# Gate and up of three feed-forward chunks by seven block products, with the sums on GpSimd

## The chip, the core and the metric

One core of a Trainium2 chip runs the whole kernel. Its engines work side by side: TensorE (PE: matrix products into PSUM; PEld is its weight load), VectorE (DVE) and ScalarE (ACT) for what comes out of PSUM and for preparing operands, GpSimd (POOL) for small things that lie in SBUF, SyncE (SP) for most of the DMA issues. The metric is the device time of one execution in microseconds.

## The reference

Two layers, each a feed-forward block, a mixer and a second feed-forward block, over 256 rows of 1024 in fp32. The mixers (latent attention with a recurrence in layer 0, differential attention in layer 1) stand outside the change. What the change touches:

```python
def swiglu(x, w_gate, w_up, w_down):
    return (jax.nn.silu(x @ w_gate) * (x @ w_up)) @ w_down

for l in range(DEPTH):
    g = norm_g[l]
    h = swiglu(rms_norm(x, g[0, 0]), ffn_w_gate[l, 0], ffn_w_up[l, 0], ffn_w_down[l, 0])
    x = x + 0.5 * rms_norm(h, g[0, 1])
    ...                                   # the mixer
    h = swiglu(rms_norm(x, g[2, 0]), ffn_w_gate[l, 1], ffn_w_up[l, 1], ffn_w_down[l, 1])
    x = x + 0.5 * rms_norm(h, g[2, 1])
```

`w_gate` and `w_up` are 1024 x 2816, `w_down` 2816 x 1024, different in each of the four blocks.

## The kernel before

The 256 rows are two tiles of 128. A product in fp32 is made of three TensorE instructions on split operands: every operand is the sum of a high part `hi` and a low part `lo`, both of type fp32r, and `mm3` (L242) issues hi x hi, hi x lo, lo x hi. The stationary operand is the transposed activation of a tile (`xT[t]`, hi and lo, for gate and up; `hT[t]` for down), the moving operand 512 columns of a weight.

**Weight stream.** Weights come in one packed array in the order of use, cut into units and these into subunits of 128 x 1024 (for gate and up two k tiles of 512 columns). `emit_load` (L197) issues for each subunit the DMA into a `raw` buffer (SP's queue; 5 buffers, L175 `wraw`), ScalarE's copy raw to `whi` (L219) and VectorE's `wlo = raw - whi` (L224), and chains the low parts so that they run in this order. In a feed-forward block split subunits lie in a pool of 7 buffers (`fw`, L422, `BUFS_F`); a mixer's, and the first of a following block, in one of 5 (`wsp`). A buffer is free again when the last product that reads it is done. `fill` (L256) keeps the stream up to seven subunits ahead of what the products have taken.

**A feed-forward block** (`ffn`, L430) runs over six chunks of the 2816 columns, of 512, 512, 256, 512, 512, 512. Each chunk multiplies both tiles by gate (`group`, L263: a subunit serves tile 0 and then tile 1, 12 instructions), evicts with silu on ScalarE (L440), multiplies by up, and forms `h` on VectorE (`gated`, L445). The transposes of the previous chunk's `h` (`turn`, L448, split by ScalarE L360 and VectorE L361) stand between gate and up, the products of the previous chunk with `w_down` behind up. The first chunk (`group_first`, L275) works on tile 0 first, because the norm and the transposes of tile 1 (`post_norm` L376, `turn_x` L363) are still under way; the down products of the last two chunks (the tail) are ordered so that the first tile's norm and transposes run beside the second tile's products.

**PSUM** is eight banks: four (`y`) hold the running down sums, four (`w`) rotate for everything else. GpSimd's work is the powers of the norms (L343, L388) and some products of the mixers. Instructions of an engine run in the order that the scheduler of the framework gave them; an engine waits at the head of its queue.

## Time and profile before

| what | us |
|---|---|
| runs | 1028.34, 1028.74, 1030.66 |
| median | 1028.74 |
| span of the profiled execution | 1027.8 |
| TensorE busy in it | 1011.3 |
| VectorE, ScalarE, GpSimd busy | 625.8, 517.1, 49.9 |

The span counts from the first to the last instruction of the execution that the hardware profiler took. In the rows further down, `L244` is a line of the program, `out<-in` are the program's tile names, `x` behind an entry is a count; what stands in brackets is the idle time of the engine just before an instruction and what ended it. Busy times of TensorE are modelled ends of pipelined instructions, so the distance between starts is the better measure of its pace.

### The profile page before, as it was taken

Reading aid. Unit: us, or ns where it says so; the run is one execution under the profiler, and the core shown is the slowest. Engines: PE = TensorE matmul, PEld = TensorE weight load, DVE = VectorE, ACT = ScalarE, POOL = GpSimd, SP = SyncE. Lnnn points to the kernel's source line nnn. Section 1 sums busy time; section 2 is a strip of 40 time slices with the busy share of each in tenths; the row PEclk is TensorE's granted clock in tenths of the full one; section 3 lists DMA queues with packets and bytes.
Section 4 is the critical chain, followed back from the end, with each engine's and each line's share of the span. In section 5 each row is a group of like instructions: output and inputs, shape, how many; then the busy total and the mean of one; then the engine's idle time right before and its main releaser. Section 6 shows DMA issues by size and latency. Waiting matters only on the chain.

```text
span 1027.8 us, 13158 instructions
## 1 busy us (share of the span) xinstructions
PE 1011.3 (98%) x4979; PEld 843.5 (82%) x4979; DVE 625.8 (61%) x876; ACT 517.1 (50%) x757; POOL 49.9 (5%) x61
## 2 busy tenths in 40 slices
PE   8999999999999999999999999999999999999997
PEld 6888888888788889888888888888877878888886
DVE  6555585768577855455576555546676786455553
ACT  6544455477644644444554444444665565444441
POOL 1000000021201000000000000000011200000000
PEclk8999999999999999999999999999999999999999
DMA  8765555575221765555547555555634366655531
GB/s 282 271 202 186 186 184 189 180 225 194 86 81 58 253 212 196 185 184 187 182 164 246 187 183 189 191 190 168 208 121 147 102 206 225 201 182 189 186 123 41
DMA packets 51903, 184.25 MB, mean 179 GB/s; under 512 B 6136, under 2 KB 6528, under 8 KB 51840
## 3 DMA queue, kind: packets, MB, share of 16 engines
q1 hardware_dynamic: 48960, 176.05, 51.8%
q10 hardware_dynamic: 2880, 7.37, 2.1%
q8 instruction: 39, 0.64, 0.2%
q14 instruction: 24, 0.20, 0.1%
HBM read 182.35 MB, written 1.05 MB: 178 GB/s over the span
## 4 chain that ended last, share of the span: by engine, by line
PE 90%; DVE 4%; issue 3%; ACT 1%; DMA 1%; POOL 1%; SPq 0%; DVEq 0%; POOLq 0%; ACTq 0%
PE w L244 16%; PE w L246 16%; PE w L245 16%; PE y L246 9%; PE y L244 9%; PE y L245 9%; PE w L292 7%; PE w L353 2%; DVE wlo L224 1%; PE y L353 1%; DMA raw<-in_w_dram 1%; ACT whi L219 1%; POOL pm L1007 0%; DVE E L857 0%; DVE pm L1009 0%
## 5 line engine op out<-in xcount | busy, mean ns | idle before, releaser
L224 DVE TENSOR_TENSOR wlo<-raw,whi 128x1024 fp32r<-128x1024 f32 (+2 forms) x331 | 404.0, 1227 | 283.6 <-ACT whi L219 281.2
L219 ACT CAST whi<-raw 128x1024 fp32r<-128x1024 f32 (+1 forms) x331 | 345.0, 1049 | 365.5 <-PE w L246 206.6
L244 PE MATMUL w<-whi,xThi 128*128 128x512 f32 (+1 forms) x836 | 315.6, 377 | 0.0
L246 PE MATMUL w<-whi,xTlo 128*128 128x512 f32 (+1 forms) x836 | 312.0, 373 | 0.0
L245 PE MATMUL w<-wlo,xThi 128*128 128x512 f32 (+1 forms) x836 | 311.5, 373 | 0.0
L246 PEld LDWEIGHTS w<-whi,xTlo 128*128 128x128 f32 x836 | 157.3, 188 | 28.3 <-issue 0.3
L244 PEld LDWEIGHTS w<-whi,xThi 128*128 128x128 f32 x836 | 157.5, 188 | 27.5 <-issue 1.0
L245 PEld LDWEIGHTS w<-wlo,xThi 128*128 128x128 f32 x836 | 157.5, 188 | 26.4
L244 PE MATMUL y<-whi,hThi 128*128 128x512 f32 x352 | 138.4, 393 | 0.0
L246 PE MATMUL y<-whi,hTlo 128*128 128x512 f32 x352 | 137.2, 390 | 0.0
L245 PE MATMUL y<-wlo,hThi 128*128 128x512 f32 x352 | 137.1, 389 | 0.0
L246 PEld LDWEIGHTS y<-whi,hTlo 128*128 128x128 f32 x352 | 66.1, 188 | 14.0
L245 PEld LDWEIGHTS y<-wlo,hThi 128*128 128x128 f32 x352 | 66.1, 188 | 13.2
L244 PEld LDWEIGHTS y<-whi,hThi 128*128 128x128 f32 x352 | 66.1, 188 | 13.2
L361 DVE TENSOR_TENSOR hTlo<-w,hThi 128x512 fp32r<-128x512 f32 (+1 forms) x48 | 29.1, 640 | 34.0 <-ACT hThi L360 34.0
L440 ACT ACTIVATE s<-w,sm 128x512 f32<-128x512 f32 (+1 forms) x48 | 31.4, 653 | 25.9 <-PE w L246 20.3
L388 POOL TENSOR_TENSOR sm<-sm,mhalf 128x1 f32<-128x1 f32 x12 | 6.6, 550 | 726.6 <-DVE sm L386 726.6
L292 PE MATMUL w<-whi,xThi 128*128 128x512 f32 (+2 forms) x124 | 39.1, 397 | 2.6 <-ACT xThi L360 2.6
L292 PE MATMUL w<-wlo,xThi 128*128 128x512 f32 (+2 forms) x124 | 37.8, 389 | 0.4 <-DVE wlo L224 0.4
L292 PE MATMUL w<-whi,xTlo 128*128 128x512 f32 (+2 forms) x124 | 37.9, 390 | 0.0
L445 DVE SCALAR_TENSOR_TENSOR h<-w,sm,s 128x512 f32<-128x512 f32 (+1 forms) x48 | 32.0, 699 | 0.7 <-PE w L246 0.5
L292 PEld LDWEIGHTS w<-whi,xThi 128*128 128x128 f32 x124 | 22.6, 192 | 6.6 <-ACT xThi L360 3.1
(246 smaller groups left out, 820.2 us busy)
## 6 DMA issues: line engine op xcount, KB each, us to landing
raw<-in_w_dram SPq DMA_DIRECT2D x325, 512.0 KB, 3.6
g<-in_norm_g_dram ACTq DMA_DIRECT2D x9, 512.0 KB, 4.6
raw<-in_w_dram SPq DMA_DIRECT2D x4, 448.0 KB, 3.4
g<-in_norm_g_dram SPq DMA_DIRECT2D x2, 512.0 KB, 6.2
out_dram<-x SPq DMA_DIRECT2D x4, 256.0 KB, 2.1
E<-in_hw_dram ACTq DMA_DIRECT2D x1, 576.0 KB, 6.7
x<-in_x_dram SPq DMA_DIRECT2D x2, 256.0 KB, 3.0
x<-in_x_dram SPq DMA_DIRECT2D x1, 512.0 KB
```

Of the source, the lines that this page charges most:

```text
L219: c = nc.scalar.copy(hi[:, :w], raw[:, :w])
L224: state["lo"] = nc.vector.tensor_tensor(lo[:, :w], raw[:, :w], hi[:, :w].bitcast(F32), op=ALU.subtract)
L244: mm(ps, hi[:, j, :], rhi, start=start, stop=False)
L245: mm(ps, hi[:, j, :], rlo, start=False, stop=False)
L246: state["mm"] = mm(ps, lo[:, j, :], rhi, start=False, stop=stop)
L292: state["mm"] = mm(o, lhs[:, k, :], rhs[:, i, :], start=j == 0 and k == 0, stop=j == 2 and k == KD - 1)
L353: nc.tensor.transpose(ps[:, i * P:(i + 1) * P], src[:, (b + i) * P:(b + i + 1) * P], ident)
L361: return c, nc.vector.tensor_tensor(lo.rearrange("p a b -> p (a b)"), ps, h2.bitcast(F32), op=ALU.subtract)
L388: nc.gpsimd.tensor_tensor(r, v, mhalf[:, :1], op=ALU.pow)
L440: nc.scalar.activation(s[:, :w], ps[:, :w], AF.Silu, scale=r[t])
L445: nc.vector.scalar_tensor_tensor(hh[:, :w], ps[:, :w], r[t], s[:, :w], op0=ALU.mult, op1=ALU.mult)
```

## The change

In chunks 1, 3 and 5 of each block the four products (tile 0, tile 1) x (gate, up) over 1024 rows of weight are seen as a product of two 2 x 2 block matrices: A11, A12 are the first and second half (512) of tile 0's columns, A21, A22 of tile 1's; B11, B21 the halves of gate, B12, B22 of up. Eight block products of 12 instructions become seven (Winograd's form), with sums of blocks as operands:

- operand sums, once a block: S1 = A21 + A22, S2 = S1 - A11, S3 = A11 - A21, S4 = A12 - S2, made on GpSimd from hi + lo (4 additions, 4 sums), then split by ScalarE's copy and GpSimd's subtraction. S1 and S2 lie in `oT`, S3 and S4 in new tiles.
- weight sums, per chunk: T1 = B12 - B11, T2 = B22 - T1, T3 = B11 - T2, T4 = B21 - T2, each as two GpSimd operations on 128 x 1024 raw weights, written over a raw buffer that is no longer needed. They go through the same split as a loaded subunit, so a chunk has 14 subunits to split, not 8, of which each serves one product of 6 instructions.
- the products in the order X = A11 B11, W = S1 T1, X += S2 T2, Y = A12 B21, X += S3 T3, X += A22 T4, W += S4 B22. ScalarE copies X to SBUF after the first, second and third product on it (`held`), VectorE adds Y or W to these copies (`plus`). tile 0's gate is X's first state + Y, tile 0's up the second + W, tile 1's up the third + W as it stands before S4 B22 is added, tile 1's gate X's last state.

The seven's raw weights get a pool of 8 buffers (`RAWS`), the feed-forward blocks' split buffers fall from 7 to 4 and alternate with the 5 of `wsp` (`RING`). Half of the previous chunk's down products stand between T3 and T4 (in the last such chunk none).

```diff
-BUFS_F = 7
+BUFS_F = 4
+SEVEN = (1,3,5)
+RAWS = 8
+RING = "wfwfwfwfw"
 ...
+        if ci in SEVEN:
+            gate, up = ([("ffn_w_" + n, (l, j), k, 4, [(a, a + w)]) for k in (0, 4)] for n in ("gate", "up"))
+            pa, pw = starts[ci - 1]
+            d = [("ffn_w_down", (l, j), f, 2, [(0, D)]) for f in range(pa // P, (pa + pw) // P, 2)]
+            half = (len(d) + 1) // 2 if ci < len(CHUNKS) - 1 else 0
+            units += [gate[0] + ("B11",), up[0] + ("T1",), up[1] + ("T2",), gate[1] + ("B21",), (None, None, 0, 4, [(a, a + w)], "T3")]
+            units += d[:half] + [(None, None, 0, 4, [(a, a + w)], "T4"), (None, None, 0, 4, [(a, a + w)], "B22")] + d[half:]
+            continue
 ...
     def emit_load():
 ...
+                raw = (wraw if kind is None else state["raws"]).tile([P, SPLIT], F32, name="raw", tag="raw")
+                moved = nc.sync.dma_start(raw[:, :w], src[:, k * nc_:k * nc_ + w])
 ...
+                sub = nc.gpsimd.tensor_tensor
+                if kind in ("B11", "B21"):
+                    kept[kind, k] = raw
+                elif kind == "T1":
+                    sub(raw, raw, kept["B11", k], op=ALU.subtract)
+                    kept["T", k] = raw
+                elif kind == "T2":
+                    kept["B22", k] = raw
+                    sub(kept["T", k], raw, kept["T", k], op=ALU.subtract)
+                    raw = kept["T", k]
+                elif kind == "T3":
+                    raw = kept["B11", k]
+                    sub(raw, kept["T", k], raw, op=ALU.subtract)
+                elif kind == "T4":
+                    raw = kept["B21", k]
+                    sub(raw, raw, kept["T", k], op=ALU.subtract)
+                else:
+                    raw = kept["B22", k]
+            pool, tag = wsp, "w"
+            if ours:
+                if RING[state["turn"] % len(RING)] == "f":
+                    pool, tag = state["pool"], "f"
+                state["turn"] += 1
 ...
+            def row_sums(fp):
+                xf = [cp.tile([P, D], F32, name="xf", tag="c") for _ in range(NT)]
+                A = [[xf[t][:, 512 * i:512 * i + 512] for i in range(2)] for t in range(NT)]
+                tt = nc.gpsimd.tensor_tensor
+                for t in range(NT):
+                    for i in range(2):
+                        hi, lo = (v.rearrange("p k n -> p (k n)").bitcast(F32) for v in half(t, i))
+                        tt(A[t][i], hi, lo, op=ALU.add)
+                tt(A[1][1], A[1][0], A[1][1], op=ALU.add)
+                tt(A[1][0], A[0][0], A[1][0], op=ALU.subtract)
+                tt(A[0][0], A[1][1], A[0][0], op=ALU.subtract)
+                tt(A[0][1], A[0][1], A[0][0], op=ALU.subtract)
 ...
+                for v, dst in zip((A[1][1], A[0][0], A[1][0], A[0][1]), (oT[0], oT[1], *more)):
+                    hi, lo = (d.rearrange("p k n -> p (k n)") for d in dst)
+                    nc.scalar.copy(hi, v)
+                    tt(lo, v, hi.bitcast(F32), op=ALU.subtract)
 ...
+            def seven(ci):
 ...
+                X = bank()
+                prod(X, half(0, 0), True)
+                hT = [turn(0, CHUNKS[ci - 1]), None]
+                W = bank()
+                prod(W, S1, True)
+                p1 = held(X)
+                hT[1] = turn(1, CHUNKS[ci - 1])
+                prod(X, S2, False)
+                Y = bank()
+                prod(Y, half(0, 1), True)
+                u2 = held(X)
+                s0 = silu(0, plus(p1, Y), 512)
+                prod(X, S3, False)
+                downs(range(kf))
+                u3 = held(X)
+                c22 = plus(u3, W)
+                prod(X, half(1, 1), False)
+                s1 = silu(1, X, 512)
+                prod(W, S4, False)
+                h = [gated(0, plus(u2, W), s0, 512), gated(1, c22, s1, 512)]
+                downs(range(kf, wp))
 ...
+            sums = row_sums(fp)
             for ci in range(1, nch):
                 w, wp = CHUNKS[ci], CHUNKS[ci - 1]
+                if ci in SEVEN:
+                    seven(ci)
+                    continue
 ...
-    nc = _bacc.Bacc("TRN2", target_bir_lowering=False, num_devices=1)
+    nc = _bacc.Bacc("TRN2", target_bir_lowering=False, num_devices=1, dynamic_dma_scratch_size=512)
```

## Rows read from the trace of the kernel before

**Rows 1.** Page, part 1: busy time, share of the span, instructions of each engine.

```profile
PE 1011.3 (98%) x4979; PEld 843.5 (82%) x4979; DVE 625.8 (61%) x876; ACT 517.1 (50%) x757; POOL 49.9 (5%) x61
```

**Rows 2.** Page, part 4: the chain that ended last, by engine.

```profile
PE 90%; DVE 4%; issue 3%; ACT 1%; DMA 1%; POOL 1%; SPq 0%; DVEq 0%; POOLq 0%; ACTq 0%
```

**Rows 3.** Timeline, TensorE: start us, us, engine, line, operation, operands, count.

```profile
553.50 0.39 PE L244 MATMUL w<-whi,xThi 128*128 128x512 f32 x1
...
576.18 0.39 PE L244 MATMUL y<-whi,hThi 128*128 128x512 f32 x1
...
587.06 0.28 PE L244 MATMUL w<-whi,xThi 128*128 128x256 f32 x1
```

**Rows 4.** Busy time by stretch, third feed-forward block: length, engines, clock, DMA.

```profile
553.50:587.10 33.60, 33.60 (x154) 27.89 (x153) 19.75 (x19) 15.18 (x17) 0.00 (x0) 1.00 0.66 222
587.10:610.20 23.10, 23.10 (x153) 21.25 (x152) 11.88 (x12) 10.22 (x12) 0.00 (x0) 1.00 0.55 181
...
638.00:671.50 33.50, 33.50 (x153) 27.80 (x153) 17.30 (x16) 14.89 (x16) 0.00 (x0) 1.00 0.58 189
...
sum 187.20, PE 187.20 PEld 157.29 DVE 105.76 ACT 88.55 POOL 2.20; mean PE 26.74 PEld 22.47 DVE 15.11 ACT 12.65 POOL 0.31
```

**Rows 5.** Timeline, VectorE, chunk 5 of that block; in brackets idle before, releaser.

```profile
675.60 1.23 DVE L224 TENSOR_TENSOR wlo<-raw,whi 128x1024 fp32r<-128x1024 f32 x1 [1.50 <-ACT whi L219]
678.32 1.23 DVE L224 TENSOR_TENSOR wlo<-raw,whi 128x1024 fp32r<-128x1024 f32 x1 [1.50 <-ACT whi L219]
```

**Rows 6.** Groups by shape: busy us, mean ns of one, idle before, releaser.

```profile
L224 DVE TENSOR_TENSOR wlo<-raw,whi 128x1024 fp32r<-128x1024 f32 x325 | 398.3, 1231 | 283.6 <-ACT whi L219 281.2
L219 ACT CAST whi<-raw 128x1024 fp32r<-128x1024 f32 x325 | 340.2, 1053 | 362.0 <-PE w L246 206.6 <-PE y L246 101.9 <-issue 24.5
...
L445 DVE SCALAR_TENSOR_TENSOR h<-w,sm,s 128x512 f32<-128x512 f32 x40 | 28.1, 742 | 0.0
...
L361 DVE TENSOR_TENSOR hTlo<-w,hThi 128x512 fp32r<-128x512 f32 x40 | 26.1, 685 | 28.4 <-ACT hThi L360 28.4
...
L360 ACT CAST hThi<-w 128x512 fp32r<-128x512 f32 x40 | 21.7, 588 | 4.7 <-PE w L353 4.6
```

**Rows 7.** The same groups for GpSimd.

```profile
L708 POOL TENSOR_TENSOR E<-E,lbm 128x512 f32<-128x512 f32 x2 | 2.6, 1290 | 4.8 <-DVE kk L707 4.8
...
L791 POOL TENSOR_TENSOR pm<-pm,sm 128x1024 f32<-128x1024 f32 x1 | 1.9, 1896 | 6.1 <-DVE sm L790 6.1
...
L847 POOL TENSOR_TENSOR XC<-E,hqT 128x256 f32<-128x256 f32 x2 | 1.7, 826 | 24.5 <-ACT E L838 24.5
```

**Rows 8.** Timeline, VectorE and GpSimd where they meet, in the two mixers.

```profile
234.80 1.37 POOL L709 TENSOR_TENSOR E<-lb,E 128x512 f32<-128x512 f32 x1
234.93 2.32 DVE L224 TENSOR_TENSOR wlo<-raw,whi 128x1024 fp32r<-128x1024 f32 x1
...
763.99 0.68 DVE L999 TENSOR_REDUCE sm<-y 128x2 f32<-128x512 f32 x1
764.10 1.04 POOL L1007 TENSOR_TENSOR pm<-pm,sm 128x512 f32<-128x512 f32 x1 [7.15 <-DVE rp L570]
...
770.17 1.23 DVE L224 TENSOR_TENSOR wlo<-raw,whi 128x1024 fp32r<-128x1024 f32 x1
770.32 1.97 POOL L1007 TENSOR_TENSOR pm<-pm,sm 128x512 f32<-128x512 f32 x1 [5.18 <-DVE sm L1006]
```

**Rows 9.** Timeline, VectorE, first and third block, around tile 1's operand.

```profile
18.87 0.69 DVE L361 TENSOR_TENSOR xTlo<-c,xThi 128x512 fp32r<-128x512 f32 x1
...
35.20 1.40 DVE L445 SCALAR_TENSOR_TENSOR h<-w,sm,s 128x512 f32<-128x512 f32 x2
...
532.63 0.75 DVE L394 SCALAR_TENSOR_TENSOR x<-c,sm,x 128x512 f32<-128x512 f32 x1
...
539.31 0.69 DVE L361 TENSOR_TENSOR xTlo<-y,xThi 128x512 fp32r<-128x512 f32 x1 [2.10 <-ACT xThi L360]
541.21 6.90 DVE L224 TENSOR_TENSOR wlo<-raw,whi 128x1024 fp32r<-128x1024 f32 x6 [1.20 <-ACT whi L219]
```

More of the change, by code (lines that the diff above doesn't have):

```diff
@@ L191, in forward @@
     SPLIT = 1024
-    state = {"i": 0, "off": 0, "block": -1, "pool": None, "first": None, "n": 0}
+    state = {"i": 0, "off": 0, "block": -1, "pool": None, "first": None, "n": 0, "turn": 0}
     queue = []
@@ L200, in emit_load @@
         u = UNITS[state["i"]]
-        pool, tag = (state["pool"], "f") if BLOCK_OF[state["i"]] == state["block"] else (wsp, "w")
+        ours = BLOCK_OF[state["i"]] == state["block"]
         state["i"] += 1
@@ L204, in emit_load @@
         nk = u[3]
-        off = state["off"]
-        state["off"] += P * width
-        src = a["w"][off:off + P * width].rearrange("(p n) -> p n", p=P)
+        kind = u[5] if len(u) > 5 else None
+        if u[0] is not None:
+            off = state["off"]
+            state["off"] += P * width
+            src = a["w"][off:off + P * width].rearrange("(p n) -> p n", p=P)
         nc_ = width // nk
@@ L212, in emit_load @@
             w = n * nc_
-            raw = wraw.tile([P, SPLIT], F32, name="raw", tag="raw")
-            moved = nc.sync.dma_start(raw[:, :w], src[:, k * nc_:k * nc_ + w])
-            if state["n"] in late:
-                after(late[state["n"]](), moved)
+            if u[0] is not None:
+                raw = (wraw if kind is None else state["raws"]).tile([P, SPLIT], F32, name="raw", tag="raw")
+                moved = nc.sync.dma_start(raw[:, :w], src[:, k * nc_:k * nc_ + w])
+                for key in [key for key in late if key <= state["n"]]:
+                    after(late.pop(key)(), moved)
+            if kind is not None:
+                sub = nc.gpsimd.tensor_tensor
[21 more added lines that the diff above has]
+                state["turn"] += 1
             hi = pool.tile([P, SPLIT], F32R, name="whi", tag=tag + "hi")
@@ new lines, in prod, with held, plus, downs @@
+            def prod(ps, lhs, start):
+                k0 = 0
+                while k0 < 4:
+                    fill()
+                    hi, lo, m, _ = queue.pop(0)
+                    for i in range(m):
+                        k = k0 + i
+                        mm3(ps, lhs, k, hi[:, i, :], lo[:, i, :], start and k == 0, k == 3, not start)
+                    k0 += m
+                    pump()
+            def seven(ci):
+                nonlocal h, hT
+                wp = CHUNKS[ci - 1] // P
+                kf = (wp // 2 + 1) // 2 * 2 if ci < nch - 1 else 0
+                wp = wp if ci < nch - 1 else 0
+                S1, S2, S3, S4 = sums
+                def held(ps):
+                    c = fp.tile([P, 512], F32, name="u", tag="u", bufs=2)
+                    nc.scalar.copy(c, ps)
+                    return c
+                def plus(c, ps):
+                    nc.vector.tensor_tensor(c, ps, c, op=ALU.add)
+                    return c
+                def downs(ks):
+                    for k in ks:
+                        sub = take(1)
+                        for t in range(NT):
+                            down(t, sub, 0 if ci == 1 else None, None, k)
+                X = bank()
[19 more added lines that the diff above has]
+                downs(range(kf, wp))
```

23 lines of the change are left out of this document (17 added, 6 removed).

## The prediction

> **What bounds the kernel now.** I read the page first. TensorE is busy for 98% of the span, VectorE for 61%, ScalarE for 50%, GpSimd for 5% [rows 1], and the chain that ended last is 90% TensorE [rows 2]: the order of questions is how much TensorE work goes, then what the other engines do with the new work. A busy share of TensorE isn't its peak, so I took the pitch from the timeline: the 48 products of 512 columns between 576.18 and 587.06 start 10.88 us apart in all, so one every 0.2267 us [rows 3], without a gap and at a granted clock of 1.00 [rows 4]. TensorE is the bound in a feed-forward block, and a product less is 0.2267 us less as long as its operands are there.
>
> Then I cut the third feed-forward block (the one between 530.9 and 718.1) into its six chunks and its tail [rows 4]. TensorE never stops there; VectorE works 105.8 of 187.2 us. In the steady stretch it does one weight low part in 1.23 us and then waits 1.50 us for ScalarE's copy [rows 5], because a buffer of the split weights comes free only every 2.72 us (12 products). So there is slack beside TensorE, but the change spends it.
>
> **The change, part by part.** *Removed.* In chunks 1, 3 and 5 of each block 7 block products of 12 instructions take the place of 8. That is 12 x 0.2267 = 2.72 us a chunk, 8.2 us a block, 32.6 us in four blocks. The down products, the transposes and the DMA bytes stay.
>
> *Added, per block.* Such a chunk consumes 14 split subunits, not 8: 18 more copies at 1.053 us on ScalarE (19.0 us) and 18 more low parts at 1.231 us on VectorE (22.2 us) [rows 6]. Three evictions to `u` and three adds from PSUM a chunk are 9 copies at 0.588 us (5.3 us) and 9 adds at about 0.685 us (6.2 us), by the rows of the same size; four copies for the operand sums add 2.4 us [rows 6]. On GpSimd come 24 weight sums of 1024 columns and 12 operand operations of 512. The latter cost 1.29 us each [rows 7]. No row shows the former with two full operands: from 256 columns (0.83) to 512 (1.29) the step is 0.46 us, so 1024 is an estimate of 2.22 us; the 1024-column row, whose second operand is a broadcast, sets the lower bound 1.90, twice the 512 row the upper, 2.58 [rows 7]. I take 2.22: same kind of operands. That makes 53.3 + 15.5 = 68.8 us of GpSimd.
>
> Sums per block, against 187.2 - 8.2 = 179.0 us of TensorE: ScalarE 88.6 + 26.7 = 115 us, VectorE 105.8 + 28.4 = 134 us, GpSimd 2.2 + 68.8 = 71 us [rows 4, 6, 7]. Each alone is covered.
>
> *The two are not independent.* A GpSimd operation of 1.04 us took 1.97 us when it started 0.15 us behind a VectorE low part: it ended 0.89 us after that one. The other way round a low part of 1.23 us took 2.32 us behind a GpSimd operation, ending 1.08 us after it [rows 8]. They run one after the other, with 0.15 us saved at each hand-over. A VectorE reduction that reads PSUM was not held by GpSimd (0.68 us beside a running 1.04 us operation) [rows 8]. So the added sums and the low parts share one resource: VectorE and GpSimd together have 134 + 71 - 36 x 0.30 (hand-overs) = 194.3 us a block if nothing else overlaps, and 171 us if the 23.3 us of VectorE work that has one operand in PSUM (12 low parts of h, 12 gatings, 9 adds) runs beside the sums. The first is above 179, the second below. No row shows an operation with one operand in PSUM and one in SBUF beside GpSimd; I take it as free, nearest to the reduction's row.
>
> The Trainium skill (SBUF — State Buffer, section Who interferes with whom) says that a VectorE instruction with at most one SBUF input, outside the two-port modes, doesn't contend with GpSimd. By it the sum is 171 us a block; without it, 194.3.
>
> *First chunk of each block: the dear place.* The operand sums need tile 1's operand, whose last low part ends at 540.00 [rows 9]; chunk 1 begins at 553.50 [rows 3, 4], and its fifth product, on T3, needs the second half of T3 split 4 products, two sets of transposes (0.6 us) and 6 instructions later: 553.5 + 10.9 + 0.6 + 1.4 = 566.4. In these 26.4 us the shared resource must do one add, four sums and three low parts for the operands (8 x 1.14 = 9.1 us), T2 and T3 (4 x 2.07 = 8.3 us), and 9 to 13 low parts at 1.08 (9.7 to 14.0 us; 13 if the last of chunk 0 must wait for buffers, as the six that start at 541.21 do [rows 9]). That is 27.1 to 31.4 us. Then T4's two sums take turns with the two down subunits that come next: 4.1 us less one product set, 1.4 us. So 2 to 6.5 us are lost a block, and up to 9 if the turns leave a tenth unused; below zero can't be, as nothing else shortens the products. I take 4.0, near the lower end, as in the first block the operand is ready 16 us ahead and not 13.5: 16 us in four blocks.
>
> *Later chunks.* The sums for chunks 3 and 5 can be made during chunks 2 and 4: 8 x 2.07 + 16 x 1.08 = 33.8 us of the shared resource against 23.1 us (chunk 2) and 33.5 us (chunk 4) [rows 4]. What is missing in chunk 2 is made up in chunk 3, where TensorE needs a subunit only every 1.36 us. I cost them at nothing; the cover is the store of nine split buffers, and without it each costs up to 10 us.
>
> *Waits added.* A product that adds onto the evicted bank waits for ScalarE's copy (0.59 us plus a copy of 1.05 in front); other products of 2.72 us stand between, except in chunk 5, ahead of T4, where up to 1.3 us lies open: zero to 5 us in all, taken as 0, since the last product can go first. A low part of a sum waits for GpSimd, and behind it on VectorE stand the next low parts, the adds and the gating, for which TensorE waits only after the store is empty. The powers of the norms queue behind sums on GpSimd, up to 2.2 us; TensorE waits for them through silu only.
>
> *Buffers and block starts.* Split buffers fall from 7 + 5 to 4 + 5. At five changes of block the next weights are split later, at most one subunit (1.4 us) short. And at the start of three blocks two operand adds (1.14 us each) can hold the norm's VectorE chain, which begins at 532.63 [rows 9] and on which tile 1 hangs. Together 0 to 14 us; I take 6. SP issues the 8 loads of a chunk into buffers of their own, so the down loads behind them wait for little.
>
> **The sum.** The profiled execution spans 1027.8 us, 0.9 below the median 1028.74. 1027.8 - 32.6 + 16 + 6 = 1017.2; with 0.9 around it 1018.1.
>
> **Rivals.** *A, all of it is hidden.* The turns in chunk 0 go to the sums early enough. For it: VectorE idles 1.5 of 2.7 us in the steady stretch [rows 5]. Against it: the 26.4 us above. 1028.7 - 32.6 = 996, with a few us lost 996 to 1006.
>
> *B, the shared resource becomes the bound: slower.* The place is the turn-taking of sums and low parts from chunk 0 to chunk 3, the price 194.3 - 187.2 = 7.1 us a block if none of the PSUM-side work overlaps: 1028.7 + 28.4 = 1057. It decides from the point where under 7.1 of the 23.3 us overlap. For it: VectorE takes its work in order, and a low part that waits for its sum holds the adds behind it, so that the two idle in turn. Against it: sums depend on raw weights only and can run ahead. I expect 1031 to 1057 from it. The skill's page named above states the mechanism as a rule: an exclusive lock, the second to issue blocks until the first is done. The two held operations [rows 8] agree with that.
>
> *C, a draw.* Stalls of 28 to 35 us: 1026.7 to 1030.8. Here too falls the case that the sums are scheduled so late in every block that a chunk's gain is its wait.
>
> **Numbers.** My forecast (1006 to 1026) 0.45, A 0.20, C 0.08, B 0.27. Within 0.2% (2.1 us) is about what a measurement of this kernel can tell from no change. Faster 0.65, same 0.08, slower 0.27. The range runs from 1000 (inside A) to 1046 (inside B).
>
> **What would show it.** Right: 144 products fewer at a pitch of 0.2267 us; TensorE's idle time in chunk 1 of each block, ended by a low part or an operand sum, 2 to 9 us; little in chunks 3 and 5; low parts and sums stretched to over 2 and 3 us where they meet. Wrong: TensorE waiting for low parts in chunks 2 to 5 (B), weight sums far from 2.2 us, or adds from PSUM stretched beside GpSimd.

## The result, and the profile after

The changed kernel takes 1128.82 us in the median of four runs (1122.55 to 1129.96), against 1028.97 (1028.34 to 1030.66) for the kernel before beside it: a ratio of 1.095, 95% interval 1.092 to 1.099. It is 100 us slower; the forecast was 11 us faster, and the range ended at 1046. The profiled execution is the one of 1122.55 us, with a span of 1120.8 us at a mean granted clock of 0.961 (before: 1027.8 us at 0.996).

The page of the changed kernel: busy time by engine, and the chain that ended last, which answer to [rows 1] and [rows 2].

```profile
PE 1007.6 (90%) x4835; PEld 825.0 (74%) x4835; DVE 860.5 (77%) x984; ACT 608.6 (54%) x881; POOL 422.1 (38%) x205
...
PE 50%; DVE 19%; POOL 13%; issue 11%; ACT 4%; DMA 3%; SPq 0%; DVEq 0%; POOLq 0%; ACTq 0%
```

The 144 products are gone (4979 instructions of TensorE before, 4835 now). Three numbers account for the span. TensorE's idle time is 1120.8 - 1007.6 = 113.2 us, where it was 16.5: 96.7 more. Its busy time is 1007.6 us, where 1011.3 - 32.6 = 978.7 was due: 28.9 more. 96.7 + 28.9 - 32.6 = 93.0, the whole difference of the two spans. Of the 28.9 us some 18 are products at the lower clock, by an estimate from the trace: TensorE is busy for 42.3 us in stretches with a granted clock of 0.50, against 6.4 us before, and at the full clock these would be half. The rest is not attributed; a part is the modelled end of the last product ahead of each wait, which counts with 0.39 us and not with its 0.2267.

The timeline of TensorE shows nearly half of the idle time in four places, one in each feed-forward block, ahead of the transposes of `h` in chunk 1 (in brackets the idle time, and what ended it):

```profile
57.74 0.87 PE L400 MATMUL w<-ident,h 128*128 128x128 f32 x3 [17.32 <-DVE h L494]
...
415.74 0.87 PE L400 MATMUL w<-ident,h 128*128 128x128 f32 x3 [9.96 <-DVE h L494]
...
627.51 1.09 PE L400 MATMUL w<-ident,h 128*128 128x128 f32 x4 [14.13 <-DVE h L494]
...
950.64 0.66 PE L400 MATMUL w<-ident,h 128*128 128x128 f32 x2 [12.21 <-ACT whi L266]
```

That is 53.6 us. The last row names a copy, but the gating of tile 0 ended later than that copy (at 950.54) and just ahead of the transposes, so this stop is of the same kind. The third block shows how such a stop comes about. GpSimd's timeline (L524 adds hi and lo, L525 to L528 are the operand sums, L534 their low parts, L249 makes T2 and L253 T3):

```profile
597.08 1.29 POOL L524 TENSOR_TENSOR xf<-xThi,xTlo 128x512 f32<-128x512 f32 x1 [2.54 <-DVE xTlo L408]
598.45 2.15 POOL L525 TENSOR_TENSOR xf<-xf 128x512 f32<-128x512 f32 x1
...
607.26 4.50 POOL L534 TENSOR_TENSOR oTlo<-xf,oThi 128x512 fp32r<-128x512 f32 x2
611.73 3.47 POOL L534 TENSOR_TENSOR Slo<-xf,Shi 128x512 fp32r<-128x512 f32 x2
615.16 2.33 POOL L249 TENSOR_TENSOR raw<-raw 128x1024 f32<-128x1024 f32 x1
617.57 2.34 POOL L253 TENSOR_TENSOR raw<-raw 128x1024 f32<-128x1024 f32 x1
619.87 3.32 POOL L249 TENSOR_TENSOR raw<-raw 128x1024 f32<-128x1024 f32 x1
```

VectorE's in the same time:

```profile
597.84 15.01 DVE L271 TENSOR_TENSOR wlo<-raw,whi 128x1024 fp32r<-128x1024 f32 x7 [0.83 <-ACT whi L266]
618.61 2.39 DVE L271 TENSOR_TENSOR wlo<-raw,whi 128x1024 fp32r<-128x1024 f32 x1 [5.76 <-ACT whi L266]
624.30 2.40 DVE L271 TENSOR_TENSOR wlo<-raw,whi 128x1024 fp32r<-128x1024 f32 x1 [3.31 <-ACT whi L266]
626.63 1.40 DVE L494 SCALAR_TENSOR_TENSOR h<-w,sm,s 128x512 f32<-128x512 f32 x2
```

and ScalarE's:

```profile
617.53 1.99 ACT L266 CAST whi<-raw 128x1024 fp32r<-128x1024 f32 x2 [9.57 <-POOL raw L249]
623.23 3.88 ACT L266 CAST whi<-raw 128x1024 fp32r<-128x1024 f32 x4 [3.71 <-POOL raw L249]
```

Read them backwards. TensorE waits for the gating of `h` (626.63). The gating stands in VectorE's queue behind T2's second low part (624.30), which waits for ScalarE's copy (623.23), which waits for GpSimd's second half of T2 (619.87). GpSimd began T2 at 615.16 only, since all operand operations stood ahead of it, and it put T3's first half between the halves of T2. While it worked through that queue, VectorE stood still for 5.76 and 3.31 us, ScalarE for 9.57 and 3.71. The loads stopped too, and the clock fell, as the stretches show (length, then busy time of PE, PEld, DVE, ACT, POOL, the granted clock, the DMA share, GB/s):

```profile
600.00:610.00 10.00, 10.00 (x46) 8.28 (x45) 10.00 (x5) 4.77 (x8) 9.76 (x6) 1.00 0.49 159
610.00:620.00 10.00, 3.38 (x15) 2.45 (x14) 4.24 (x3) 1.99 (x2) 9.92 (x6) 0.79 0.00 0
620.00:630.00 10.00, 2.49 (x8) 2.23 (x9) 6.69 (x6) 5.73 (x7) 6.25 (x3) 0.50 0.00 0
630.00:640.00 10.00, 10.00 (x41) 8.09 (x41) 10.00 (x8) 6.81 (x9) 5.89 (x2) 0.85 0.45 143
```

0.50 is the lower of TensorE's two clocks, 1.2 GHz. The products behind the stop come 0.43 us apart (timeline of TensorE), where 0.2267 is the pitch of [rows 3]:

```profile
628.83 0.63 PE L292 MATMUL w<-wlo,oThi 128*128 128x512 f32 x1
629.25 0.63 PE L293 MATMUL w<-whi,oTlo 128*128 128x512 f32 x1
629.68 0.63 PE L291 MATMUL w<-whi,oThi 128*128 128x512 f32 x1
```

The groups by shape answer to [rows 6, 7]: a low part has gone from 1231 to 1577 ns on the mean, weight sums take 2.9 to 3.3 us, and the adds from PSUM (L564) are not stretched:

```profile
L271 DVE TENSOR_TENSOR wlo<-raw,whi 128x1024 fp32r<-128x1024 f32 x397 | 613.8, 1577 | 148.2 <-ACT whi L266 146.7
...
L256 POOL TENSOR_TENSOR raw<-raw 128x1024 f32<-128x1024 f32 x24 | 79.0, 3310 | 24.4 <-DVE wlo L271 19.5 <-ACT hThi L407 3.7 <-ACT whi L266 1.2
...
L249 POOL TENSOR_TENSOR raw<-raw 128x1024 f32<-128x1024 f32 x24 | 69.0, 2874 | 196.5 <-DVE wlo L271 196.5
...
L564 DVE TENSOR_TENSOR u<-w,u 128x512 f32<-128x512 f32 x36 | 24.5, 681 | 0.0
```

Two smaller losses come back. At the start of the third block, on GpSimd, two weight sums stand ahead of the power of the norm (L435), and later two operand adds hold the norm's VectorE work, so that TensorE waits 2.99 us (3.06 at the start of the second):

```profile
571.89 4.75 POOL L245 TENSOR_TENSOR raw<-raw 128x1024 f32<-128x1024 f32 x2 [29.00 <-DMA raw<-in_w_dram]
576.60 0.55 POOL L435 TENSOR_TENSOR sm<-sm,mhalf 128x1 f32<-128x1 f32 x1
...
590.70 0.63 PE L400 MATMUL y<-ident,xg 128*128 128x128 f32 x4 [2.99 <-DVE xg L447]
```

In chunk 5 of every block the copy of a bank to `u` stands behind other work on ScalarE; in the third:

```profile
762.39 0.62 PE L291 MATMUL w<-whi,xThi 128*128 128x512 f32 x1 [1.79 <-ACT u L560]
```

One longer stop stands alone, in chunk 3 of the first block:

```profile
142.98 0.79 PE L292 MATMUL w<-wlo,xThi 128*128 128x512 f32 x1 [4.71 <-DVE wlo L271]
```

VectorE came to that low part (141.71) behind, among others, a low part in turns with a sum (3.43 us) and a reciprocal of the mixer (3.34 us).

From the first product of the third block to the first of what follows are 208.4 us, where [rows 4] has 187.2. By stages, against before: chunk 0 +4.8 us, the stop in chunk 1 +14.1, the rest of chunk 1 +5.3 (2.4 of it clock), chunk 3 +1.1, chunk 5 and the tail +4.1, products -8.2. In the four blocks, counted from the first product of chunk 1 to the first of chunk 2, chunk 1 lost 24.2, 18.1, 19.3 and 20.2 us beyond its saving of 2.72: 81.8 of the 125.6 us (93.0 + 32.6) that the change lost against its saving.

### The profile page after: what moved, and what is told of

It is laid out like the page before. It is cut to its first block, busy times and chain, and to the rows that moved or that the text cites. A ratio compares the mean times of both kernels' runs of the same rounds, so it can differ in the third digit from the quotient of the medians.

```text
span 1120.8 us, 13313 instructions
## 1 busy us (share of the span) xinstructions
PE 1007.6 (90%) x4835; PEld 825.0 (74%) x4835; DVE 860.5 (77%) x984; ACT 608.6 (54%) x881; POOL 422.1 (38%) x205
## 4 chain that ended last, share of the span: by engine, by line
PE 50%; DVE 19%; POOL 13%; issue 11%; ACT 4%; DMA 3%; SPq 0%; DVEq 0%; POOLq 0%; ACTq 0%
DVE wlo L271 12%; PE w L291 9%; PE w L293 9%; PE w L292 9%; PE y L291 5%; PE y L293 5%; PE y L292 5%; PE w L339 3%; DMA raw<-in_w_dram 3%; POOL raw L249 3%; ACT whi L266 2%; PE w L400 1%; POOL xf L524 1%; DVE x L441 1%; DVE u L564 1%
## 5 line engine op out<-in xcount | busy, mean ns | idle before, releaser
L271 DVE TENSOR_TENSOR wlo<-raw,whi 128x1024 fp32r<-128x1024 f32 (+1 forms) x403 | 619.8, 1568 | 149.9 <-ACT whi L266 148.3
L266 ACT CAST whi<-raw 128x1024 fp32r<-128x1024 f32 (+1 forms) x403 | 413.9, 1048 | 310.8 <-DMA raw<-in_w_dram 80.9
L291 PE MATMUL w<-whi,xThi 128*128 128x512 f32 (+1 forms) x596 | 223.4, 375 | 18.4 <-ACT u L560 13.9
L292 PE MATMUL w<-wlo,xThi 128*128 128x512 f32 (+1 forms) x596 | 219.5, 368 | 6.3 <-DVE wlo L271 6.3
L293 PE MATMUL w<-whi,xTlo 128*128 128x512 f32 (+1 forms) x596 | 219.2, 368 | 0.0
L291 PEld LDWEIGHTS w<-whi,xThi 128*128 128x128 f32 x596 | 112.8, 189 | 42.9 <-ACT u L560 18.5
L249 POOL TENSOR_TENSOR raw<-raw 128x1024 f32<-128x1024 f32 x24 | 69.0, 2874 | 196.5 <-DVE wlo L271 196.5
L292 PEld LDWEIGHTS w<-wlo,xThi 128*128 128x128 f32 x596 | 112.9, 189 | 24.5 <-DVE wlo L271 7.6
L293 PEld LDWEIGHTS w<-whi,xTlo 128*128 128x128 f32 x596 | 112.9, 189 | 19.1 <-issue 0.3
L245 POOL TENSOR_TENSOR raw<-raw 128x1024 f32<-128x1024 f32 x24 | 70.0, 2927 | 143.6 <-DMA raw<-in_w_dram 126.5
L256 POOL TENSOR_TENSOR raw<-raw 128x1024 f32<-128x1024 f32 x24 | 79.0, 3310 | 24.4 <-DVE wlo L271 19.5
L400 PE MATMUL w<-ident,h 128*128 128x128 f32 x176 | 27.7, 287 | 53.7 <-DVE h L494 41.4
L253 POOL TENSOR_TENSOR raw<-raw 128x1024 f32<-128x1024 f32 x24 | 69.1, 2883 | 1.4
L435 POOL TENSOR_TENSOR sm<-sm,mhalf 128x1 f32<-128x1 f32 x12 | 6.6, 550 | 103.4 <-DVE sm L433 103.4
```

Source lines behind the costliest of these rows:

```text
L245: sub(raw, raw, kept["B11", k], op=ALU.subtract)
L249: sub(kept["T", k], raw, kept["T", k], op=ALU.subtract)
L253: sub(raw, kept["T", k], raw, op=ALU.subtract)
L256: sub(raw, raw, kept["T", k], op=ALU.subtract)
L266: c = nc.scalar.copy(hi[:, :w], raw[:, :w])
L271: state["lo"] = nc.vector.tensor_tensor(lo[:, :w], raw[:, :w], hi[:, :w].bitcast(F32), op=ALU.subtract)
```

## The experiments

Differences below are medians minus the median of the kernel before in the same comparison. Theory Q: TensorE waits because results come late through queues served in order. Theory P: the turns that GpSimd and VectorE take stretch VectorE's work until TensorE waits. (In the first four expectations these are the order theory, in e3 the theory of the first chunk, and the port theory.)

| run | us | ratio (95%) | difference |
|---|---|---|---|
| the change | 1128.8 | 1.095 (1.092 to 1.099) | +99.9 |
| e1, gating ahead of T2's low parts | 1121.1 | 1.088 (1.084 to 1.092) | +90.7 |
| e2, all sums on VectorE | 1037.6 | 1.007 (1.005 to 1.009) | +7.2 |
| e3, chunks 3 and 5 alone | 1077.0 | 1.046 (1.043 to 1.049) | +46.6 |
| e4, no operand sums | 1075.1 | 1.044 (1.041 to 1.046) | +44.7 |
| e5, buffers alone | 1033.7 | 1.004 (1.003 to 1.005) | +4.0 |
| e6, sums that nobody reads | 1081.0 | 1.049 (1.046 to 1.052) | +51.3 |
| e7, weight sums on VectorE | 1058.1 | 1.027 (1.025 to 1.030) | +28.5 |
| e8, operand sums on VectorE | 1097.6 | 1.064 (1.061 to 1.068) | +67.9 |
| e9, e6 with sums behind the norms | 1080.4 | 1.047 (1.045 to 1.049) | +49.3 |
| e10, chunks 3 and 5 on VectorE | 1027.1 | 0.995 (0.993 to 0.997) | -4.0 |
| e11, e10 with late operand sums | 1019.4 | 0.988 (0.986 to 0.990) | -11.7 |
| e12, e3 with late operand sums | 1075.5 | 1.043 (1.041 to 1.045) | +44.5 |
| e13, e6 with the order forced | 1076.1 | 1.045 (1.043 to 1.046) | +45.9 |
| e14, e11 with chunk 4 too | 1056.8 | 1.027 (1.023 to 1.030) | +26.6 |
| e15, e12 with the order forced | 1083.9 | 1.053 (1.051 to 1.055) | +53.7 |
| e16, operand operations, unread | 1053.7 | 1.022 (1.020 to 1.025) | +23.6 |
| e17, and 24 private sums a block | 1058.4 | 1.028 (1.025 to 1.030) | +28.3 |
| e18, and 48 private sums a block | 1144.2 | 1.112 (1.108 to 1.115) | +114.1 |

**e1: the gating first.** T2's low parts are issued on VectorE behind the gating of chunk 0's `h`.

```diff
+            if kind == "T2":
+                state.setdefault("t2", []).append(state["lo"])
 ...
+            for lo2 in state.pop("t2", []):
+                after(lo2, state["h"])
```

> Only an order: in the first chunk of each block the low parts of T2 are issued behind the two gatings of h, not ahead of them. Theory order (the stop of 10 to 17 us ahead of the transposes of h is made by the gating standing in VectorE's queue behind a low part that waits for T2, which waits on GpSimd for the twelve operand operations): the stop goes from that place, a shorter one of 3 to 9 us appears ahead of the product on T2, and 5 to 8 us a block come back: 1096 to 1108 us. Theory port (GpSimd and VectorE simply have too much for one shared resource, whatever the order): T2 and what follows come no earlier, at most 8 us come back in all, 1120 us or more.

It gave back 9 us of 100; the time lies in the port theory's range. The stop of the third block only moved, by two sets of transposes and a product, to the product on T2 (timelines of this run, TensorE and ScalarE):

```profile
629.52 0.79 PE L293 MATMUL w<-whi,oThi 128*128 128x512 f32 x1 [10.27 <-ACT u L562]
...
625.10 3.88 ACT L266 CAST whi<-raw 128x1024 fp32r<-128x1024 f32 x4 [3.71 <-POOL raw L249]
628.89 0.57 ACT L562 COPY u<-w 128x512 f32<-128x512 f32 x1
```

The place of the gating is not the cause. T2 is late, and whatever TensorE needs first behind T2 is what it waits for; here it is the copy to `u`, which stands on ScalarE behind four copies of weights, the first of them waiting for GpSimd.

**e2: all sums on VectorE.** One word in two places:

```diff
-                sub = nc.gpsimd.tensor_tensor
+                sub = nc.vector.tensor_tensor
 ...
-                tt = nc.gpsimd.tensor_tensor
+                tt = nc.vector.tensor_tensor
```

> All sums (24 weight sums, 12 operand operations a block) move from GpSimd to VectorE, all else as in the change. By the rows of before a weight sum costs 1.2 us there, an operand operation 0.69 us: 37 us a block, VectorE 171 of 179 us. Theory port: the two engines' turns are gone, the low parts fall from 1.58 us back to 1.23 us, and the time falls to 1005 to 1035 us. Theory order alone (the queue order is what costs): the low part of T2 still stands ahead of the gating, but its chain is 12 x 0.69 us and not 12 x 2.15 us, so 40 to 60 us come back: 1070 to 1090 us.

93 of the 100 us come back, with the same products, sums, splits, buffers and copies. The page of this run and its group of low parts:

```profile
PE 994.9 (96%) x4835; PEld 818.8 (79%) x4835; DVE 856.1 (83%) x1128; ACT 609.2 (59%) x881; POOL 53.0 (5%) x61
...
L271 DVE TENSOR_TENSOR wlo<-raw,whi 128x1024 fp32r<-128x1024 f32 x397 | 476.2, 1225 | 64.3 <-ACT whi L266 62.2
```

VectorE is as busy as in the change (856 us against 860): its sums cost it what the turns had cost it. So the loss is GpSimd's. The time is 2.6 us above the port theory's range and far below that of the order theory. It is not yet said whether it is GpSimd's pace and queue, or the turns.

**e3 and e4: less of it.** e3 leaves chunk 1 at eight products (`SEVEN = (3,5)`). e4 multiplies by parts of the operands in place of their sums, so its result is another one:

```diff
-            sums = row_sums(fp)
+            sums = [half(1, 0), half(1, 1), half(0, 0), half(0, 1)]
```

> Seven products in chunks 3 and 5 only; chunk 1 has eight, so the operand sums have some 50 us until they are needed. TensorE saves 21.8 us and not 32.6. Theory first chunk (the loss lies between the norm of tile 1 and the end of chunk 1): what stays is the later chunks' waits and the block starts, 1025 to 1045 us. Theory port: the sums cost in every chunk, two thirds of the loss of 125 us stay, 1085 to 1095 us.

> The twelve operand operations a block and their four copies are left out; the products take halves of the operand that lie there already, so the output is not the reference's. Weight sums stay on GpSimd. Theory order: T2 follows T1 at once, the stops ahead of the transposes go nearly all, and 60 to 75 us come back: 1053 to 1068 us. Theory port: GpSimd sheds 26 us of 104 us a block, so a quarter of the loss comes back, about 1098 us.

Both give back a little over half and leave some 45 us, between what the theories expected. Neither the first chunk alone nor the operand operations alone are the cause.

**e5 and e6: the buffers, and sums that nobody reads.** e5 has `SEVEN = ()` and no operand operations. e6 adds GpSimd's load, written to tiles that nothing reads:

```diff
+                if kind == "idle":
+                    sub(state["unread"], raw, raw, op=ALU.subtract)
```

> All chunks by eight products as in the kernel before, no sums of weights or operands anywhere; only what the change does to the weight buffers stays (the short ring that alternates between the two pools, the pool of eight raw tiles). Theory Q (TensorE waits for results that come late through GpSimd's queue) and theory P (the turns of GpSimd and VectorE stretch VectorE's work) both expect 1026 to 1034 us, the time of before. A third theory, that the shorter ring starves the low parts, expects 1040 us or more, and would take as much out of the share of the other two.

> As the run with the buffers alone, all products by eight, but GpSimd carries the load of the change: 24 sums of 128x1024 per block, one behind each raw tile of chunks 1, 3 and 5, and the 12 operations of 128x512 on the operands behind chunk 0. They are written to tiles that nothing reads, so nobody waits for them; raw tiles come free later, as in the change. Theory P (turns): the mean of a low part goes from 1231 ns to about 1550, gating and the norms wait behind them, and the time is 1060 to 1100 us. Theory Q (waits for results): low parts are as slow, but VectorE and ScalarE have room for it, the time is 1028 to 1042 us, and no stop of TensorE above 3 us stands ahead of the transposes of h.

The buffers cost 4.0 us. The unread sums cost 47 us more, which spoke for P. But the trace shows where: of four stops over 5 us, two (6.61 and 6.62) end with the norm at the start of a block, one (6.33) with a low part of a first chunk, one (5.21) with the gating ahead of chunk 1, and in chunks 2 to 5 none reaches 1 us. The third block's (timelines, GpSimd and TensorE):

```profile
542.95 16.57 POOL L243 TENSOR_TENSOR unread<-raw 128x1024 f32<-128x1024 f32 x8 [82.96 <-PE w L402]
559.47 0.55 POOL L437 TENSOR_TENSOR sm<-sm,mhalf 128x1 f32<-128x1 f32 x1
...
561.59 1.11 PE L402 MATMUL y<-ident,xg 128*128 128x128 f32 x4 [6.61 <-DVE xg L449]
```

The power of a norm, half a microsecond, stood behind eight sums of this block's weights. VectorE waited 8.94 us for it, and TensorE 6.61. So nobody read the sums, and yet something waited behind them.

**e7 and e8: one kind of sums at a time.** Each makes one of the two changes of e2.

> The change with the 24 weight sums of a block on VectorE, the 12 operand operations left on GpSimd. Theory Q: T2 no longer stands behind the operand operations, its hi copies are early; what is left is the chain of four adds, four sums and four low parts on GpSimd (about 1.3 to 2.2 us each, some 16 to 20 us from tile 1's operand), of which the first operand sum is needed 3 us into chunk 1: a stop of 4 to 7 us per block with its clock, 1055 to 1072 us. Theory P: only a fifth of GpSimd's columns are left, 1045 to 1055 us.

> The change with the 12 operand operations of a block on VectorE (about 0.7 us each), the 24 weight sums left on GpSimd. Theory Q: T2 stands behind T1 alone and is done some 10 us earlier; 4 to 6 us of each stop are left, and the waits of chunk 5 stay, 1065 to 1085 us, near the 1075 of the run that left the operand sums out. Theory P: four fifths of GpSimd's columns still take turns, so at most a fifth of the 91 us that both moves together gave comes back: 1105 to 1115 us. If the shares of this run and of the run with the weight sums on VectorE add up to more than 91 us, the two kinds of sums cost by standing in one queue.

The weight sums' share is 99.9 - 28.5 = 71.4 us, the operand operations' 99.9 - 67.9 = 32.0. Together 103.4, while both moves together gave 92.7: 10.7 us are paid only because both stand on GpSimd.

**e9, e13, e15: another order on GpSimd.** e9 emits the sums of chunk 1 behind the operand operations in the program; e13 and e15 force it, for all sums of a block, by an order on GpSimd (`rows` the last operand operation, in e15 the last power of the norms).

```diff
+            for s_ in state["held"]:
+                after(s_, state["rows"])
```

> As the run in which nobody reads GpSimd's sums (all products by eight, 24 sums of 128x1024 and 12 operations of 128x512 per block on GpSimd, 1081 us), but the eight sums beside the weights of chunk 1 are given to GpSimd behind the operand operations, so that no sum of the block stands ahead of the powers of the norms at its start. The load and the turns with VectorE stay the same. Theory Q (GpSimd's queue is served in order, and what TensorE needs stands behind the sums): the stops of 6 us at the start of a block go, 1034 to 1048 us, while the mean of a low part stays near 1600 ns. Theory P (the turns cost, wherever they fall): 1070 to 1085 us.

> The run in which nobody reads GpSimd's sums (all products by eight, 1081 us), with an order forced: every sum beside the weights of a block is issued behind the last of the operand operations, and so behind the powers of the norms at the block's start. Theory Q (the powers stand behind the sums in GpSimd's queue): the stops of 6.6 and 6.3 us at block starts go, 1034 to 1046 us, with low parts still near 1600 ns on the mean. Theory P (turns with VectorE cost wherever they fall): 1070 to 1085 us, and the stops move into chunk 1 or later.

> Seven products in chunks 3 and 5, all sums on GpSimd, operand sums issued in chunk 1, as in the run of 1075.5 us, but every weight sum of a block is issued behind the last power of the norms at its start. Theory Q: the block starts and chunk 1 are free of stops, the waits for u copies in chunks 3 and 5 (about 4 us a block with their half clock some 6) stay, 1035 to 1050 us. Theory P: 1065 to 1078 us.

In e9 the framework's scheduler took the sums forward again; GpSimd's timeline has all eight of chunk 1 (six of the loop, L614, and two of L244) ahead of the power, so the run tells nothing:

```profile
542.12 12.62 POOL L614 TENSOR_TENSOR unread<-raw 128x1024 f32<-128x1024 f32 x6 [81.60 <-PE w L405]
554.81 3.86 POOL L244 TENSOR_TENSOR unread<-raw 128x1024 f32<-128x1024 f32 x2
558.63 0.55 POOL L440 TENSOR_TENSOR sm<-sm,mhalf 128x1 f32<-128x1 f32 x1
```

In e13 the order holds, the stops of 6.6 us are gone, and 5.4 of the 51.3 us come back. Q, as I had put it (only the powers stand behind the sums), is wrong. The raw tiles are now held until GpSimd comes to them, loads start late, and ScalarE waits for one with everything that stands behind it (timeline of ScalarE):

```profile
605.62 1.05 ACT L270 CAST whi<-raw 128x1024 fp32r<-128x1024 f32 x1 [12.79 <-DMA raw<-in_w_dram]
```

e15 is worse than e12 by 9 us. Early, the sums hold the norms; late, they hold the raw tiles.

**e16, e17, e18: the turns alone.** All products by eight, with the change's buffers. e16 has the 12 operand operations, unread. e17 and e18 add 24 and 48 sums a block on tiles of their own: no raw tile is held, no power stands behind them.

```diff
+            def load_pool(n, ci):
+                u = state["unread"]
+                if ci:
+                    nc.gpsimd.tensor_tensor(u[:, :256], h[1][:, :256], h[1][:, :256], op=ALU.subtract)
+                for _ in range(n):
+                    nc.gpsimd.tensor_tensor(u, xf, u, op=ALU.add)
```

> All products by eight with the change's buffers (1033.7 us with the buffers alone), plus the 12 operand operations of 128x512 per block on GpSimd, which nobody reads; no sums of weights. Theory P (the turns alone cost): low parts of chunk 0 and 1 are stretched by some 12 turns of about 1 us, a stop of up to 3 us per block, 1036 to 1050 us. Theory Q (only what stands behind GpSimd's work costs): 1034 to 1038 us.

> As the run with operand operations only, plus 24 sums of 128x1024 per block on GpSimd on tiles of their own, eight each behind the gating of chunks 0, 2 and 4, the same columns as the change. Nothing waits for them, they hold no raw tile, and no power of a norm stands behind them. Theory P: the share of the 47 us that belongs to the turns shows here, 1060 us or more, the low parts near 1600 ns. Theory Q: low parts near 1600 ns too, but 1034 to 1045 us.

> As the run with 24 sums on private tiles, with 48 per block. Theory P: twice the loss, 1085 us or more. Theory Q: as long as a chunk's low parts in turns (12 of about 2.2 us and the gating, some 30 us) fit into a chunk of 33 us of TensorE, little more than with 24: 1036 to 1055 us.

The groups of low parts and private sums, first of e17 and then of e18:

```profile
L272 DVE TENSOR_TENSOR wlo<-raw,whi 128x1024 fp32r<-128x1024 f32 x325 | 602.4, 1884 | 97.5 <-ACT whi L267 95.8
L615 POOL TENSOR_TENSOR unread<-xf,unread 128x1024 f32<-128x1024 f32 x96 | 314.2, 3272 | 7.2
```

```profile
L272 DVE TENSOR_TENSOR wlo<-raw,whi 128x1024 fp32r<-128x1024 f32 x325 | 739.0, 2314 | 49.7 <-ACT whi L267 48.8
L615 POOL TENSOR_TENSOR unread<-xf,unread 128x1024 f32<-128x1024 f32 x192 | 607.1, 3162 | 14.7
```

In e17 the low parts are slower than in the change (1884 ns against 1577), and the 24 sums cost 4.7 us over e16. Behind the gating of chunks 0, 2 and 4 the turns cost next to nothing, because VectorE has the room. It has more of it than in the change: with eight products it is spared the 28.4 us a block that the prediction added for it. No run puts unread sums beside the change's whole VectorE work. With 48 the room is used up and 86 us more are lost: at 445 us five low parts take 3.33 us each in turns, and the split of `h` behind them (hTlo) comes so late that TensorE waits 8.21 us for it (timelines of e18):

```profile
443.54 16.65 DVE L272 TENSOR_TENSOR wlo<-raw,whi 128x1024 fp32r<-128x1024 f32 x5
460.12 1.27 DVE L409 TENSOR_TENSOR hTlo<-w,hThi 128x512 fp32r<-128x512 f32 x2
...
460.85 0.79 PE L294 MATMUL y<-whi,hTlo 128*128 128x512 f32 x1 [8.21 <-DVE hTlo L409]
```

e16 is the surprise: 12 short operations a block cost 19.6 us, five a block, since they fall where VectorE has no room. At the start of the third block two adds in turns stretch the norm (timelines of VectorE and TensorE; the first row took 0.74 us without GpSimd beside it):

```profile
540.70 1.77 DVE L442 SCALAR_TENSOR_TENSOR x<-c,sm,x 128x512 f32<-128x512 f32 x1
542.40 2.30 DVE L272 TENSOR_TENSOR wlo<-raw,whi 128x1024 fp32r<-128x1024 f32 x1
...
545.45 0.87 PE L401 MATMUL y<-ident,xg 128*128 128x128 f32 x4 [2.10 <-DVE xg L448]
```

**e10, e11, e12, e14: a version that gains.** e10 and e3 have `SEVEN = (3,5)`, e14 `SEVEN = (3,4,5)`; e10, e11 and e14 have the sums on VectorE, e12 on GpSimd. e11, e12 and e14 issue the operand sums in chunk 1:

```diff
-            sums = row_sums(fp)
 ...
                 hT = [turn(t, wp) for t in range(NT)]
+                if ci == 1:
+                    sums = row_sums(fp)
```

> Seven products in chunks 3 and 5 alone, all sums on VectorE. 96 products of 0.2267 us less than before are 21.8 us, the buffers cost 4 us (run with the buffers alone), the eight operand operations, four low parts and 16 weight sums of a block (about 28 us) fit into VectorE's 80 us of room. Theory Q: 1010 to 1020 us, faster than before. Theory P agrees, as nothing is left on GpSimd. If chunk 1 still stops behind the operand sums on VectorE (5.3 us in the run with three chunks on VectorE), 1018 to 1030 us.

> As the run with seven products in chunks 3 and 5 and all sums on VectorE, but the operand sums are issued behind the low parts of h in chunk 1, not ahead of chunk 1. If the operand sums disturb the start of chunk 1, this is 4 to 12 us faster than that run, 1006 to 1016 us; if they don't, both are the same within 2 us.

> Seven products in chunks 3 and 5, all sums on GpSimd as in the earlier run of these two chunks (1077 us), but the operand sums are issued behind the low parts of h in chunk 1. Theory Q: the gating and the transposes of chunk 1 no longer wait; what is left are the sums of the weights of chunk 3 that stand ahead of the operand sums, and the u copies, 1040 to 1060 us. Theory P: GpSimd's columns are the same, 1070 to 1080 us.

> Seven products in chunks 3, 4 and 5, all sums on VectorE, operand sums issued in chunk 1. 48 products of 0.2267 us less than the run with chunks 3 and 5 (1019.4 us) are 10.9 us. If VectorE keeps up over three such chunks in a row: 1007 to 1013 us. If it does not (its work there, some 37 us a chunk by the groups of the run with chunks 3 and 5, stands against some 31 us of TensorE), or the eight raw tiles come free too late: 1016 to 1035 us.

e11 is faster than both kernels: 1019.4 us, 1.2% under the kernel before. Its page:

```profile
PE 993.5 (98%) x4883; PEld 823.2 (81%) x4883; DVE 788.5 (78%) x1060; ACT 584.3 (58%) x845; POOL 51.3 (5%) x61
```

96 products less are 21.8 us. By the profiles (1015.5 against 1027.8 us) 12.3 of them arrive. TensorE's idle time is 22.0 us against 16.5, and its busy time 993.5 against a due 989.5, so 9.5 us go there, as far as the page tells (e5 lost 4.0 us by the buffers alone). e10 differs by the place of 12 short operations only, and is 8 us slower; it lies in the second of its two ranges, e11 3 us above its own. e12 lies in P's range but says little on P: the operand operations are ready early, so that they ran at the same place on GpSimd as in e3. e14 shows the limit of VectorE's room: with three such chunks in a row VectorE is busy for 27.8 of 30 us (160 to 190 us), TensorE waits for copies and low parts of weights, and 27 us are lost, more than expected.

**What the 100 us are made of.** By the ranges alone neither theory is right: P's came true in e6, e9, e12, e13 and e18, Q's in e7; e8 and e17 lie between the two, e15 and e16 above both. Taken one after another: buffers +4.0 (e5); operand operations that nobody reads +19.6 (e16); weight sums in turns, unread, on tiles of their own +4.7 (e17); the same sums on the raw tiles of the stream +23.0 (e6), through the powers behind them, the tiles that they hold, or turns at the start of a block, where e17 has no weight sums; the rest, with TensorE waiting for the results, +81.2; products -32.6. The last but one is a remainder, not a run of its own, and it holds the three evictions and adds and the added splits too, with what the turns cost beside them. With the sums on VectorE, all that lies above the buffers and the products is 7.2 - 4.0 + 32.6 = 35.8 us. What part of the 23.0 is the powers', the raw tiles' and the turns' stays open, since each order that spares the powers pays with the tiles.

## Why the prediction was wrong, point by point

**The removed products: right.** 144 fewer, at the pitch of 0.2267 us wherever TensorE isn't stopped.

**The first chunk: the step that failed.** It took 4.0 us a block, 2 to 9 as bounds, 16 us in four blocks; chunk 1 lost 18 to 24 us a block and 81.8 in all, in the third block 14.1 in the stop and 5.3 around it. Two things in that step were wrong.

First, the deadline. I gave the shared resource 26.4 us, from tile 1's operand to the fifth product. TensorE takes its instructions in order, and the second thing in chunk 1 are the transposes of `h`. From tile 1's operand (597.0) to them (613.4) are 16.4 us, 10.0 less than I counted. That 4.0 + 10.0 is near the stop that came is in part luck: in the other blocks it was 10.0, 12.2 and 17.3. I had even named the order that makes it so ("behind it on VectorE stand ... the gating"), and then wrote that TensorE waits for the gating only after the store is empty. e1 shows that mending the gating alone would not have helped: the next thing in TensorE's queue that hangs on T2 is a product later.

Second, the sum. 27.1 to 31.4 us of work was counted as if the shared resource were never idle. T2's last low part ended 29.7 us behind the operand (626.7). That this lies in the range is luck, since T3, which the sum includes, was not split yet. The way was another: T2 passes GpSimd, ScalarE and VectorE in turn, each in order, and VectorE stood for 9.1 of the last 14 us. A latency was priced as a throughput. The turns have a part in it, on GpSimd's side: from 597.08 to 615.16 it did nine operations of 512 columns in 18.1 us, which at 1.29 us each would be 11.6, so by this estimate up to 6.5 us of the stop are turns that lengthened GpSimd's own queue. e7 and e8 show the queue in numbers: both kinds of sums on GpSimd cost 10.7 us that neither kind costs alone.

**Weight sums: mis-sized.** Estimated at 2.22 us (1.90 to 2.58); alone they took 2.33, but the means in the run are 2.87 to 3.31. The turns were counted for VectorE only, as something that a sum of both engines takes care of. They lengthen the chain as well.

**Block starts: mis-sized.** 6 us in all (0 to 14); e16 shows 19.6 for the operand operations alone, which includes their part in chunk 1. The mechanism was named (two adds beside the norm), its price not: the norm is followed by TensorE at once. The sentence that the powers are delayed by up to 2.2 us was short too: two sums of 4.75 us stood ahead of one in the change, eight in e6.

**Later chunks at nothing: right in the main, incomplete.** In the third block chunks 2 and 4 took the time of before. The sign of being wrong that I named, TensorE waiting for a low part in chunks 2 to 5, came once: the 4.71 us at 142.98. And the waits for `u`, taken as 0 of 0 to 5 us, came eleven times in the four blocks (up to 2.3 us each, and behind one of them products at the lower clock): 14.1 us of TensorE's waits end with that copy. The cover named, that the last product can go first, was not in the program. e2, with the same order of products, has two such waits of 2.6 us in all, so most of the 14.1 comes with the sums on GpSimd.

**The clock: not in the sum.** Some 18 us of products at the lower clock. [Rows 4] show 1.00 in all stretches of the block, because TensorE never stopped there; the price of a stop was taken as its length, without the slower products behind it.

**The rivals.** The sign was B's; the mechanism, as far as the runs show, wasn't. B priced the shared resource as a bound over the whole block (194.3 against 187.2 us, 1031 to 1057). e17 puts the price of 24 sums at 4.7 us, but beside less VectorE work than the change's, so B's sum was not tested as it stands. Against it as the main cause speaks e2, where VectorE is as busy and 93 us are gone. The adds with one operand in PSUM, on which B hung, were free, as taken. GpSimd was idle beside most of the 36; three ran wholly beside a sum and took 0.68 to 0.69 us, against 685 ns for the row of the same size in [rows 6]. One of them (timelines of VectorE and GpSimd):

```profile
130.49 0.69 DVE L564 TENSOR_TENSOR u<-w,u 128x512 f32<-128x512 f32 x1
...
128.33 6.88 POOL L245 TENSOR_TENSOR raw<-raw 128x1024 f32<-128x1024 f32 x2 [7.26 <-DMA raw<-in_w_dram]
```

The Trainium skill (SBUF — State Buffer, section Who interferes with whom) says that an instruction of VectorE with at most one SBUF input, outside its two-port modes, doesn't contend with GpSimd; these three adds agree. What B lacked is that turns cost by where they fall. A put the loss at up to 10 us and C at some 30, against the 125.6 that came; C's stalls of 28 to 35 us should read 30.6 to 34.7, by the times given with them.

## What to carry to other kernels

Price work that moves to a slow in-order engine by the path of one result through all queues up to the first waiting instruction of the bounding engine, in that engine's own order, not by the sums of busy time; and ask of each small instruction already in that queue (here the powers of the norms) who waits for it. Where that engine stops, add the products at the lower clock that follow. If work must be added beside a full engine, put it where the helper has room and nothing is due: the place of 12 short operations a block was worth 8 us (e10, e11).

## What was not expected of the hardware

- Turns are nearly one for one. A low part and a sum, 1.23 us and 2.33 us alone, took 3.3 us as a pair (16.65 us for five in e18). VectorE alone does both in less (1.23 and 1.22 us in e2), since a sum of that size takes it half of GpSimd's time.
- The granted clock went to 0.50 in the stops of 10 to 17 us, and was at 0.50 behind one wait of 1.79 us too: twelve products took 4.4 us after it (762.39 to 766.83), against 2.72. Behind two waits of 1.80 us (554.81 and 1088.08) it stayed at 1.00.
- Loads stop with their consumers: 0 GB/s from 610 to 630 us, while ScalarE waited for GpSimd's sums. That the raw tiles were all taken then is inferred from the waits, not shown by a run.
